# A two-layer decoder trunk on one core: input tiles on two pages in turns, gate rows in three bf16 parts, wider attention units, a new table of times

## The chip, the cores and the metric

The kernel runs on one core of one Trainium2 chip. The metric is the time of one launch on the device in microseconds, as the median of several runs. The core has a matmul engine (PE, with its weight loads shown apart as PEld), a vector engine (DVE), a scalar engine (ACT), a general engine (POOL) and a queue engine (SP) from which nearly all DMA transfers are issued. Each engine works through its own instructions strictly in order. Where an instruction needs something that another engine or a transfer produces, it waits at the head of its engine, and all that stands behind it waits too.

## The reference, cut to what matters

Input x is 1024 rows of 1024 f32. There are two layers. Each normalizes the rows, projects them by one wide matrix, runs three kinds of mixer on the columns, multiplies by gates, and projects back.

```python
for layer in range(DEPTH):                        # DEPTH = 2
    h = rms_norm(x, ln_g[layer])
    if layer % 2 == 0:
        u = h @ even_w_in[li]
        y_a = mla_mixer(...)                      # 8 heads, causal softmax attention
        y_b = nsa_mixer(...)                      # 8 heads in 2 groups: compressed, selected, window
    else:
        u = h @ odd_w_in[li]
        y_c = dsa_mixer(...)                      # top 256 keys of an indexer's score
        y_d = mlstm_mixer(...)                    # the recurrence, below
    y_m = mem_xattn(...)                          # 256 memory slots
    x = x + concat(y1 * silu(gate), y2 * silu(gate), y_m * silu(gate)) @ w_out[layer]
```

The recurrence of the second layer, for each of 4 heads, goes over chunks of the sequence with a state C (64x128), n and m:

```python
        b = jnp.cumsum(lfc, axis=-1)
        D = jnp.where(tril, b[..., :, None] - b[..., None, :] + ic[..., None, :], NEG)
        m_t = jnp.maximum(b + m[..., None], D.max(-1))
        a = jnp.exp(b + m[..., None] - m_t)
        w = jnp.einsum('bhtd,bhsd->bhts', qc, kc) * jnp.exp(D - m_t[..., None])
        num = a[..., None] * jnp.einsum('bhtd,bhdv->bhtv', qc, C) + jnp.einsum('bhts,bhsv->bhtv', w, vc)
```

## The kernel before, in words

The program first records every operation of the whole trunk (a recorder's `add`), then orders them with a list scheduler, and only then issues them. All instructions but a few therefore come from line 559, the one place that issues, and a profile row is told from another by the names of its tiles.

**What sets the order.** Each operation belongs to a segment, such as `norm` (normalizing the input tiles), `e_agate` (a block of columns of the first projection), `nsa`, `mlstm` or `dsa`. The table `SEG` gives each segment two times, between which its operations get their due times. The scheduler fills the five engines by these due times and by a planner's costs; some elementwise operations may go to DVE, ACT or POOL, by the weights in `PRICE`. Tiles live in pages of 4 KB or 2 KB for each partition; PSUM has 8 banks. A tile that is asked for when no page is free has to wait for the last reader of an older one.

**Precision.** A projection splits h and the weights into a high and a low f16 half, `hT` (h transposed by DMA, from `nh` and `nl`) and `wl`, so each product is three 512-column matmuls for each of 8 slices of the inner dimension. The row `wl,hT` is this work. It is also what the scheduler has at hand to fill PE while other chains run. Raw weights come in as `wr`, 512 KB at a time.

**The start** (`even`, class `Lazy`). The 8 tiles of 128 input rows come as `xt`, each on a page of its own, issued up to two tiles ahead of the one being normalized. For each tile ACT squares it (`nj`), POOL forms the scale (`ms`), ACT or DVE makes `nh` and DVE `nl`, and two DMA transposes write `hT`.

**The sparse attention** (`attention`, `units`). For each of 8 query tiles and 2 head groups, scores go into PSUM (by `u_S`), DVE reduces them to a row maximum (`nm`), ACT takes the exponential into `P`, and its high and low halves go to `PS`, which is turned into `PT` by the DMA (`PT<-PS`) or by PE. One unit is as many heads as fit in `UNIT` = 512 score columns:

```python
        n = 128 * grp["nk"] or 64
        per = max(1, min(4, UNIT // max(n, 128)))
```

**The recurrence** (`mlstm`). Gate pre-activations lie as `lf` and `ig` with positions on partitions. Sixteen small PE transposes (`cst,lf` and `cst,ig`) turn them into rows of 4 heads by 1024 positions. DVE then scans the rows; from these come `nu` (in the page `row0`) and `a` (in `row3`), both 4x1024 f32. To use a row against a 128-partition tile, a matmul with a 4-row selector `sel` spreads it over the partitions: `row,sel` 4x512 for `qa`, and 4x128 for each head and chunk of 128 positions (8 chunks), added in PSUM to a mask (`mb,idb`) before an exponential. These matmuls have f32 operands; the trace shows each as two instructions. The chunk ends with `mixB`, and the recurrence's state goes on to the next.

Of the kernel before, what the change touches and what calls it, by code (L numbers as in the profile page):

```python
# [10 lines left out]
BF = mybir.dt.bfloat16  # L11
# [14 lines left out]
PRICE = {"V": 0.6056, "S": -0.3, "G": -0.042}  # L26
# [636 lines left out]
def shape_constants():  # L663
# [8 lines left out]
    for i in range(NT):  # L672
# [8 lines left out]
SEG = dict(mem1=(-1964.354997, -749.898006), setup=(-1816.241273, -1509.540986), nsak=(-356.853517, 1584.760751), norm=(12.478188,  # L681
           60.715408), e_agate=(30.389285, 702.674675), kv0=(180.608921, 332.472885), cmp=(295.381558, 524.45868),
           late=(404.880094, 623.097485), q1=(414.776892, 755.823398), nsav=(449.064004, 909.7325), q0=(574.250466, 967.487664),
           e_kv1=(639.09141, 640.09141), e_lat=(657.807884, 810.40051), e_bgate=(702.751148, 801.565528), kv1=(719.691156,
           930.091156), e_bq=(742.856149, 985.342984), e_mq=(764.26877, 930.810665), e_kv2=(790.238444, 844.321004),
           nsa=(872.306006, 1320.680104), tab1=(879.7302, 1666.299134), mla0=(909.091866, 999.091866), mla1=(963.432059,
           1054.709671), oA0=(1011.102231, 1143.413799), mkv0=(1035.698803, 1135.060803), mem0=(1071.084555, 1249.633293),
           oBM0=(1130.594329, 1373.974849), topk1=(1192.612434, 1894.010943), o_idx=(1305.901793, 1411.398144),
           topk0=(1324.297644, 1929.352671), o_og1=(1349.47565, 1535.745353), o_cgate=(1373.820186, 1759.504578),
           o_dqk=(1519.607611, 1585.829092), o_og0=(1553.774079, 1798.172126), o_mq=(1729.947172, 1862.135725), o_cq=(1760.056059,  # L690
           1908.507699), o_dv=(1799.75511, 1904.957928), mlstm=(1813.754032, 2012.421441), mkv1=(1844.716227, 1889.690991),
           cv=(1879.3423, 2062.848758), dsa=(1890.783201, 2305.248509), oBM1=(1961.965806, 2207.495428), oA1=(2186.525082,
           2466.927226))
# [3 lines left out]
UNIT = 512  # L697
# [10 lines left out]
class Trunk:  # L708
# [457 lines left out]
    def units(self, grp):  # L1166
        n = 128 * grp["nk"] or 64
        per = max(1, min(4, UNIT // max(n, 128)))
        st = {64: 64, 128: 128, 256: 256}.get(n, 512)
        res = []  # L1170
        for a in range(0, 4, per):
            res.append(dict(grp=grp, heads=list(range(a, a + per)), n=n, st=st, first=(a == 0), last=(a + per == 4), turn=False))
        return res
# [128 lines left out]
    def attention(self, kind, groups, side=None):  # L1302

        seq = []
        for gi, g in enumerate(groups):
            g["gi"] = gi
            seq += self.units(g)
# [160 lines left out]
    def even(self):  # L1468
# [19 lines left out]
        class Lazy:  # L1488
# [3 lines left out]
            def get(s, i):  # L1492
                while s.n <= i:
                    j = s.n
                    with self.seg("norm"):
                        for y in range(len(xts), min(j + 3, NT)):
                            xts.append(self.page("xt"))
                            Q.dma_start(xts[y], A["x"][0, 128 * y:128 * y + 128])
                        hT.append(self.norm_T(xts[j], "hT"))
                    xts[j] = None  # L1500
# [772 lines left out]
    def mlstm(self, qkT, gif, dv_d, mix):  # L2273
# [79 lines left out]
        sel = self.page("sel", [128, 8, 128])  # L2353
        for h in range(4):
            V.tensor_copy(sel[0:4, h], self.idf[0:4, h:h + 1].to_broadcast([4, 128]))
        for j in range(2):
            for k in range(2):
                V.tensor_copy(sel[0:4, 4 + j, 64 * k:64 * k + 64], self.idf[0:4, 2 * j + k:2 * j + k + 1].to_broadcast([4, 64]))
        dcol = self.tiny(16, F, "dcol")
        t = self.psT()  # L2360
        for j in range(2):
            T.matmul(t[:, 8 * j:8 * j + 8], sel[0:4, 4 + j], dec[0:4], start=True, stop=True)
# [12 lines left out]
        for c in range(NT):  # L2375
# [15 lines left out]
            for h in range(4):  # L2391
                T.matmul(dps[:, 128 * h:128 * h + 128], sel[0:4, h], nu[:, tk], start=True, stop=False)
# [143 lines left out]
```

## Time and profile before

| | |
|---|---|
| median of 3 runs | 1490.56 us (1482.39, 1490.56, 1491.02) |
| profiled execution | 1491.9 us |
| its span | 1490.1 us (1.8 us lie outside) |
| mean granted clock of PE | 0.966 |
| PE, DVE busy | 1369.9 us (92%), 1270.4 us (85%) |
| ACT, POOL busy | 1077.0 us (72%), 459.0 us (31%) |

A busy share is an average over the whole program. The program has stretches with different limits, so the rows are read by stretch. [...]

### The profile page before, as it was taken

The numbers are of one execution on the slowest core, as the hardware profiler recorded it, in microseconds if no ns is written. First come the engines' busy times: TensorE is split into PE (matmuls) and PEld (weight loads), VectorE is DVE, ScalarE is ACT, GpSimd is POOL, SyncE is SP. The second block draws the span as 40 slices with busy tenths as digits, with TensorE's granted clock in tenths as the row PEclk, the third lists the DMA queues.
The fourth block names the chain that finished last, engine by engine and source line by source line (L and its number), as shares of the span: only waits on it lengthen the run. The fifth ranks groups of instructions, "written<-read, shape, count | busy, mean of one in ns | idle before, by whom it ended". The sixth has DMA issues, their size and how long they took to land. (4 is left out here: it accounts for less than half of the span.)

```text
span 1490.1 us, 30067 instructions
## 1 busy us (share of the span) xinstructions
PE 1369.9 (92%) x10496; PEld 784.3 (53%) x10496; DVE 1270.4 (85%) x3477; ACT 1077.0 (72%) x2497; POOL 459.0 (31%) x501
## 2 busy tenths in 40 slices
PE   3999999999888889978899999999998978999997
PEld 1345445556666556655656554444443455665553
DVE  7656798999989978798899899868999988988894
ACT  8545565558878968895888789999997565655580
POOL 1312355767420323341214310000266523221030
PEclk9999999999999999999999999999998897699999
DMA  9827522468498798978998332042135477369996
GB/s 304 203 78 176 162 86 88 121 144 165 99 178 162 148 218 213 246 180 156 213 221 163 87 89 75 15 135 82 36 91 143 89 124 216 82 152 244 264 244 159
DMA packets 441849, 225.49 MB, mean 151 GB/s; under 512 B 378080, under 2 KB 404320, under 8 KB 441696
## 3 DMA queue, kind: packets, MB, share of 16 engines
q1 hardware_dynamic: 441696, 223.57, 63.9%
q8 instruction: 82, 1.34, 0.4%
q14 instruction: 71, 0.58, 0.1%
HBM read 83.61 MB, written 46.66 MB: 87 GB/s over the span
## 5 line engine op out<-in xcount | busy, mean ns | idle before, releaser
L559 PE MATMUL psum<-wl,hT 128*128 128x512 f16 (+4 forms) x2928 | 662.8, 367 | 14.1 <-DMA hT<-nh 8.3
L559 PEld LDWEIGHTS <-hT 128*128 128x128 f16 x2928 | 279.5, 98 | 313.6 <-issue 29.7
L559 PEld LDWEIGHTS <-PT 128*128 128x128 f16 x3792 | 234.9, 101 | 74.5 <-DMA PT<-PS 44.3
L559 PE MATMUL psum<-wl,oT 128*128 128x512 f16 x960 | 265.6, 383 | 8.8 <-DVE oe L559 3.3
L559 POOL TENSOR_TENSOR ms<-ms,nhalf 128x4 f32<-128x4 f32 (+3 forms) x105 | 118.2, 1130 | 456.6 <-DVE ms L559 221.9
L559 ACT ACTIVATE P<-psum,nm 128x256 f32<-128x256 f32 (+8 forms) x348 | 203.1, 598 | 66.4 <-DVE nm L559 55.0
L559 PE MATMUL psum<-nv,PT 128*128 128x64 f16 x1584 | 177.0, 195 | 21.1 <-DMA PT<-PS 18.1
L559 DVE TENSOR_REDUCE nm<-psum 128x1 f32<-128x640 f32 (+8 forms) x216 | 161.9, 765 | 22.3 <-PE psum L559 21.3
L559 PEld LDWEIGHTS <-oT 128*128 128x128 f16 x960 | 93.6, 99 | 105.5 <-DMA oT<-osp 7.6
L559 DVE SCALAR_TENSOR_TENSOR PS<-P,PS 128x512 f16<-128x512 f32 (+6 forms) x160 | 129.3, 811 | 2.6 <-ACT PS L559 2.4
L559 PE MATMUL psum<-cst,P 128*128 128x128 f32 x502 | 103.3, 295 | 8.3 <-ACT P L559 4.2
L559 ACT ACTIVATE PT<-psum 128x512 f16<-128x512 f32 (+3 forms) x160 | 76.9, 507 | 38.6 <-PE psum L559 31.6
L559 PEld LDWEIGHTS <-qf 128*128 128x128 f16 x832 | 78.0, 101 | 43.5 <-issue 13.7
L559 PE MATMUL psum<-nkst,qf 128*128 128x320 f16 (+5 forms) x384 | 95.8, 320 | 4.0 <-DVE PT L559 1.6
L559 DVE SCALAR_TENSOR_TENSOR PT<-psum,PT 128x512 f16<-128x512 f32 (+3 forms) x160 | 88.1, 567 | 10.2 <-ACT PT L559 9.6
L559 ACT ACTIVATE tkj<-tkr,tkv 128x768 bf16<-128x768 f32 (+5 forms) x96 | 83.5, 872 | 14.2 <-DVE tkv L559 7.6
L559 ACT ACTIVATE PS<-P 128x512 f16<-128x512 f32 (+6 forms) x113 | 82.1, 729 | 4.2 <-PE psum L559 2.8
L559 ACT ACTIVATE wj<-wr 128x1024 bf16<-128x1024 f32 (+5 forms) x78 | 79.2, 1020 | 8.1 <-DMA wr<-even_w_in 5.2
L559 PE MATMUL psum<-vp,PT 128*128 128x64 f16 x864 | 79.0, 193 | 5.5 <-DMA PT<-PS 3.1
L559 PE MATMUL psum<-cvp,PT 128*128 128x64 f16 x864 | 78.0, 193 | 6.1 <-DMA PT<-PS 5.6
L559 DVE TENSOR_TENSOR wl<-wr,wl 128x1024 f16<-128x1024 f32 (+4 forms) x65 | 78.1, 1208 | 3.9 <-ACT wl L559 3.5
L559 ACT ACTIVATE tkj<-stop,tkd,tkf 128x1024 bf16<-128x1024 bf16 (+5 forms) x84 | 80.7, 967 | 0.1
(498 smaller groups left out, 2822.7 us busy)
## 6 DMA issues: line engine op xcount, KB each, us to landing
wr<-even_w_in SPq DMA_DIRECT2D x20, 512.0 KB, 5.0
wr<-w_out SPq DMA_DIRECT2D x20, 512.0 KB, 5.3
wr<-odd_w_in SPq DMA_DIRECT2D x20, 512.0 KB, 4.4
gate<-gate_d SPq DMA_DIRECT2D x32, 256.0 KB, 4.7
gate_d<-gu SPq DMA_DIRECT2D x24, 256.0 KB, 2.2
qa_d<-mqT SPq DMA_DIRECT2D x16, 384.0 KB, 2.6
xt<-x SPq DMA_DIRECT2D x8, 512.0 KB, 10.3
x<-x SPq DMA_DIRECT2D x8, 512.0 KB, 5.8
```

The source lines that it names most:

```text
L559: r = getattr(engines[o.eng], meth)(*[res(a) for a in args], **{k: res(v) for k, v in kw.items()})
```

## The change: what it does

There are four edits. The input tiles use two pages in turns: tile y goes into the page of tile y-2, and one tile is fetched ahead less. The two gate rows are each split into three bf16 rows whose sum is the f32 value to within what three bf16 mantissas hold (copy, subtract, copy, subtract), and the selector is bf16, so that each f32 matmul becomes three bf16 matmuls into the same PSUM columns; the small `dec,sel` matmuls stay f32. In the sparse attention alone a unit may have 1024 score columns, two PSUM banks. And `SEG` and one weight of `PRICE` have new numbers, so that all is ordered anew.

```diff
-PRICE = {"V": 0.6056, "S": -0.3, "G": -0.042}
+PRICE = {"V": 0.5977, "S": -0.3, "G": -0.042}
...
-           60.715408), e_agate=(30.389285, 702.674675), kv0=(180.608921, 332.472885), cmp=(295.381558, 524.45868),
+SEG = dict(mem1=(-2553.531656, -565.442386), setup=(-2429.265397, -2428.265397), norm=(0.251578, 91.068331), nsak=(60.696859,
...
-UNIT = 512
+UNIT = {"mla": 512, "nsa": 1024, "mem": 512, "dsa": 512}
...
-    def units(self, grp):
+    def units(self, grp, width):
         n = 128 * grp["nk"] or 64
-        per = max(1, min(4, UNIT // max(n, 128)))
+        per = max(1, min(4, width // max(n, 128)))
...
-                        for y in range(len(xts), min(j + 3, NT)):
-                            xts.append(self.page("xt"))
+                        for y in range(len(xts), min(j + 2, NT)):
+                            xts.append(xts[y - 2] if y > 1 else self.page("xt"))
                             Q.dma_start(xts[y], A["x"][0, 128 * y:128 * y + 128])
...
-        sel = self.page("sel", [128, 8, 128])
...
+        selb = self.page("selb", [128, 6, 128], BF)
+        sel = self.page("sel", [128, 2, 128])
...
+        def thirds(x):
+
+            res = [self.page("third", dt=BF)[0:4] for _ in range(3)]
+            r = self.page("rest")[0:4]
+            self.copy(res[0], x)
+            self.tt(r, x, res[0], OP.subtract)
+            self.copy(res[1], r)
+            self.tt(res[2], r, res[1], OP.subtract)
+            return res
+        nu3, a3 = thirds(nu), thirds(a)
...
             for c in range(2):
-                T.matmul(ps[:, c], sel[0:4, 4 + j], a[:, 512 * c:512 * c + 512], start=True, stop=True)
+                for x, r in enumerate(a3):
+                    T.matmul(ps[:, c], selb[0:4, 4 + j], r[:, 512 * c:512 * c + 512], start=(x == 0), stop=(x == 2))
...
-                T.matmul(dps[:, 128 * h:128 * h + 128], sel[0:4, h], nu[:, tk], start=True, stop=False)
+                for x, r in enumerate(nu3):
+                    T.matmul(dps[:, 128 * h:128 * h + 128], selb[0:4, h], r[:, tk], start=(x == 0), stop=False)
```

**The queue of SP at the program's start.** In the name of a row, the first word is the tile written, after the arrow what is read. Before, from its fifth row on (ahead of these stand one `xt`, `cst` of 82 KB, `gcol` of 27.5 KB and one `wr`):

```order
L559 DMA wr_116<-even_w_in 128x2x512
L559 DMA wr_120<-even_w_in 128x2x512
L559 DMA wr_122<-even_w_in 128x2x512
L559 DMA xt_124<-x 128x1024
L559 DMA xt_126<-x 128x1024
L559 DMA xt_133<-x 128x1024
L559 DMA xt_142<-x 128x1024
L559 DMA xt_163<-x 128x1024
L559 DMA xt_178<-x 128x1024
L559 DMA xt_183<-x 128x1024
L559 DMA_TRANSPOSE hT_187<-nh_168 128x8x128
```

And now, from its fifth row on (ahead stand `w` of 256 KB, `cst`, `gcol` and one `xt`):

```order
L559 DMA xt_116<-x 128x1024
L559 DMA wr_120<-even_w_in 128x2x512
L559 DMA wr_122<-even_w_in 128x2x512
L559 DMA wr_124<-even_w_in 128x2x512
L559 DMA wr_128<-even_w_in 128x2x512
L559 DMA posi_137<-pos 128x9
L559 DMA wr_148<-even_w_in 128x2x512
L559 DMA gb_160<-rows 128x968
L559 DMA mraw_172<-cst 128x896
L559 DMA_TRANSPOSE hT_181<-nh_177 128x8x128
L559 DMA_TRANSPOSE hT_191<-nl_179 128x8x128
L559 DMA xt_102<-x 128x1024
```

Six tiles of `x` moved from ahead of the first transpose to behind it, each after the transposes of an earlier tile, and three other loads and one weight tile moved ahead of it.

**PE where the recurrence's gates are turned into rows.** Before, the transposes of `lf` (`cst,lf`) stand among projection matmuls:

```order
L559 MATMUL psum<-wl_15247,hT_11029 128x512
L559 MATMUL psum<-cst_88,lf_13143 4x128
L559 LDWEIGHTS hT_12460
L559 MATMUL psum<-wl_14489,hT_12460 128x512
L559 MATMUL psum<-cst_88,lf_13143 4x128
L559 LDWEIGHTS hT_11713
L559 MATMUL psum<-wl_14806,hT_11713 128x512
```

Now they stand in one run (`mT` is the transposed memory, another projection's operand):

```order
L559 LDWEIGHTS mT_15256
L559 MATMUL psum<-wl_15586,mT_15256 128x512
L559 MATMUL psum<-cst_88,lf_13088 4x128 x8
L559 LDWEIGHTS hT_12551
L559 MATMUL psum<-wl_14573,hT_12551 128x512
```

Over the whole program, 2102 of the 512-column matmuls `wl,hT` and `wl,mT` stood ahead of the first of these transposes, and 2216 do now. From there to the recurrence's last chunk there were 298 of them, and 184 are there now; of the output projection's (`wl,oT`) there were 35 and are 4.

**PE at the gate rows of the first chunks.** Before, a row against the selector stands alone:

```order
L559 MATMUL psum<-row_3397_15563,sel_12929 128x128
L559 LDWEIGHTS hT_12065
L559 MATMUL psum<-wl_15184,hT_12065 128x512
L559 LDWEIGHTS idb_131
L559 MATMUL psum<-mb_429,idb_131 128x128
```

Now each of them is three matmuls with a weight load ahead of each. At the first chunk's last head the parts of `nu` (here `third_15847`, 128 columns) share a run of twelve with the parts of `a` (`third_16016` and `third_16033`, 512 columns), of which five rows are:

```order
L559 MATMUL psum<-third_16016,selb_15183 128x512
L559 LDWEIGHTS selb_15183
L559 MATMUL psum<-third_15847,selb_15183 128x128
L559 LDWEIGHTS selb_15183
L559 MATMUL psum<-third_16033,selb_15183 128x512
```

What moved is the place of `a`: its two matmuls for each of two tiles stood alone and ahead of all chunks, and their parts now stand in that run. In all, 36 f32 matmuls (32 of 128 columns, 4 of 512) became 108 bf16 matmuls, each with a weight load of its own; on DVE 8 copies of `sel` became 3, three subtractions or copies of 4x1024 were added, and ACT got four and POOL one. On DVE 264 row maxima became 244 and the DMA transposes `PT<-PS` went from 160 to 150.

## Rows read from the trace of the kernel before

**Rows 1.** The page: span, busy time by engine, and the ending chain by step.

```profile
span 1490.1 us, 30067 instructions
...
PE 1369.9 (92%) x10496; PEld 784.3 (53%) x10496; DVE 1270.4 (85%) x3477; ACT 1077.0 (72%) x2497; POOL 459.0 (31%) x501
...
PE psum L559 15%; DMA PT<-PS 2%; ACT P L559 1%; DVE PS L559 1%; DVE row L559 1%; DVE P L559 1%; ACT tkj L559 0%; POOL ms L559 0%; DMA oT<-osp 0%; DVE Cst L559 0%; DVE x L559 0%; ACT PS L559 0%; DVE tkn L559 0%; DVE tkr L559 0%; SPq L559 0%
```

**Rows 2.** Windows: stretch, length, busy time (instructions) by engine, clock, DMA, GB/s.

```profile
0.00:48.00 48.00, 21.07 (x75) 8.28 (x76) 35.58 (x132) 38.20 (x57) 6.72 (x13) 0.90 1.03 288
48.00:320.00 272.00, 269.56 (x1402) 136.86 (x1400) 209.92 (x756) 146.85 (x347) 122.84 (x142) 1.00 0.44 123
320.00:860.00 540.00, 485.64 (x5275) 321.37 (x5273) 483.80 (x1115) 434.39 (x1099) 186.37 (x228) 0.98 0.84 176
860.00:1111.00 251.00, 247.50 (x1198) 119.21 (x1196) 220.16 (x647) 236.62 (x478) 33.43 (x31) 1.00 0.24 74
1111.00:1142.00 31.00, 28.74 (x141) 13.24 (x139) 30.05 (x63) 26.33 (x56) 19.97 (x14) 1.00 0.45 147
1142.00:1200.00 58.00, 55.49 (x226) 26.74 (x227) 52.57 (x123) 29.89 (x65) 29.50 (x20) 0.82 0.40 86
1200.00:1330.00 130.00, 115.43 (x791) 75.97 (x789) 113.89 (x347) 82.53 (x233) 34.99 (x31) 0.83 0.67 148
1330.00:1490.00 160.00, 146.44 (x1404) 82.66 (x1399) 124.42 (x301) 82.24 (x168) 25.18 (x24) 1.00 0.96 224
```

**Rows 3.** PE's timeline at the start: start, length, work, idle before and releaser.

```profile
21.80 3.39 PE L559 MATMUL psum<-wl,hT 128*128 128x512 f16 x8 [8.26 <-DMA hT<-nh]
...
28.15 8.32 PE L559 MATMUL psum<-wl,hT 128*128 128x512 f16 x30
...
43.61 16.73 PE L559 MATMUL psum<-wl,hT 128*128 128x512 f16 x64 [1.80 <-DVE gu L559]
```

**Rows 4.** The tile xt: what reads it (ns min, median, max), and its landing.

```profile
L559 ACT ACTIVATE nj<-xt x8: 1038/1039/1057, 4.4 to 27.1; 128x1024 bf16<-128x1024 f32 x8
...
DMA to landing us min/median/max: 3.6/10.3/11.0
```

**Rows 5.** PE's timeline in the recurrence.

```profile
1118.81 21.10 PE L559 MATMUL psum<-wl,hT 128*128 128x512 f16 x97
1142.06 1.98 PE L559 MATMUL psum<-row,sel 4*128 4x512 f32 x4 [2.15 <-ACT row L559]
...
1238.64 0.48 PE L559 MATMUL psum<-row,sel 4*128 4x128 f32 x2
...
1255.17 0.79 PE L559 MATMUL psum<-row,sel 4*128 4x128 f32 x2 [3.87 <-DVE PT L559]
```

**Rows 6.** Windows of 4 us where the gate rows end (columns as in rows 2).

```profile
1140.00:1144.00 4.00, 1.94 (x4) 0.66 (x4) 4.00 (x4) 3.98 (x5) 4.00 (x2) 1.00 0.63 164
1144.00:1148.00 4.00, 2.21 (x5) 1.26 (x5) 4.00 (x9) 3.17 (x10) 2.26 (x3) 0.54 0.71 133
1148.00:1152.00 4.00, 3.34 (x12) 1.46 (x11) 4.00 (x11) 1.49 (x4) 0.00 (x0) 0.50 0.35 66
```

**Rows 7.** The tile row: its copy on DVE and an exponential on ACT.

```profile
L559 ACT ACTIVATE strow<-row x2: 1054/1055/1056, 1130.9 to 1143.1; 4x1024 f32<-4x1024 f32 x2
L559 DVE COPY row<-psum x1: 1202/1202/1202, 1116.7 to 1116.7; 4x1024 f32<-4x1024 f32 x1
```

**Rows 8.** Groups by shape: busy us, mean ns, idle before and releaser.

```profile
L559 POOL TENSOR_TENSOR wl<-wr,wl 128x1024 f16<-128x1024 f32 x19 | 44.1, 2323 | 35.9 <-ACT wl L559 23.7 <-PE psum L559 8.6 <-DVE wl L559 2.1
...
L559 PEld LDWEIGHTS <-idb 128*128 128x128 bf16 x248 | 24.8, 100 | 13.8 <-issue 1.8
...
L559 DVE TENSOR_REDUCE nm<-psum 128x1 f32<-128x1024 f32 x16 | 19.4, 1218 | 2.1 <-PE psum L559 1.9
...
L559 DVE TENSOR_REDUCE nm<-psum 128x1 f32<-128x512 f32 x24 | 16.1, 680 | 0.0
```

**Rows 9.** What PE waited for: total us, times, longest.

```profile
PE psum L559 <- DMA PT<-PS: 31.1, 32, 3.1
```

More of the change, by code (lines that the diff above doesn't have):

```diff
@@ L678, in shape_constants @@
     return c
-SEG = dict(mem1=(-1964.354997, -749.898006), setup=(-1816.241273, -1509.540986), nsak=(-356.853517, 1584.760751), norm=(12.478188,
-           60.715408), e_agate=(30.389285, 702.674675), kv0=(180.608921, 332.472885), cmp=(295.381558, 524.45868),
[L683 to L693, printed above, removed]
@@ new lines @@
+SEG = dict(mem1=(-2553.531656, -565.442386), setup=(-2429.265397, -2428.265397), norm=(0.251578, 91.068331), nsak=(60.696859,
+           1538.120436), e_agate=(171.33351, 771.686517), cmp=(174.284895, 488.621415), late=(175.937474, 604.970939),
+           q1=(410.702592, 450.538766), nsav=(473.233518, 937.172328), kv0=(496.192916, 834.479676), e_kv1=(503.492017,
+           610.61793), q0=(540.654991, 944.014504), e_lat=(657.807884, 810.40051), e_bgate=(696.328747, 795.143128),
+           e_bq=(742.856149, 919.882141), kv1=(747.606624, 990.444352), e_mq=(764.26877, 930.810665), e_kv2=(790.296979,
+           844.379539), nsa=(872.306006, 1320.680104), tab1=(892.840546, 1684.102713), mla0=(909.091866, 996.176523),
+           mla1=(991.127269, 1054.709671), mkv0=(1035.698803, 1135.060803), oA0=(1036.464838, 1142.292346), mem0=(1076.208498,
+           1254.757236), oBM0=(1133.782374, 1377.162893), topk1=(1195.995111, 1894.621025), o_idx=(1305.901793, 1418.004966),
+           o_og1=(1316.898953, 1539.059171), topk0=(1320.28138, 1929.352671), o_cgate=(1396.110474, 1780.678022),
+           o_dqk=(1537.749253, 1599.020946), o_og0=(1606.005922, 1805.340579), o_cq=(1674.294572, 1877.928297), o_mq=(1716.781976,
+           1853.081082), cv=(1745.740444, 2048.281883), mkv1=(1788.302893, 1889.866807), o_dv=(1798.083266, 1907.690467),
+           mlstm=(1815.433596, 2006.209633), oBM1=(1955.379054, 2245.360699), dsa=(1969.715907, 2284.982961), oA1=(2009.907991,
+           2828.098532))
@@ L1306, in attention @@
             g["gi"] = gi
-            seq += self.units(g)
+            seq += self.units(g, UNIT[kind])
         for x, u in enumerate(seq):
@@ L1495, in get @@
                     with self.seg("norm"):
-                        for y in range(len(xts), min(j + 3, NT)):
-                            xts.append(self.page("xt"))
+                        for y in range(len(xts), min(j + 2, NT)):
+                            xts.append(xts[y - 2] if y > 1 else self.page("xt"))
                             Q.dma_start(xts[y], A["x"][0, 128 * y:128 * y + 128])
                         hT.append(self.norm_T(xts[j], "hT"))
-                    xts[j] = None
                     s.n += 1
@@ L2351, in mlstm @@
         yield 1
-        sel = self.page("sel", [128, 8, 128])
[L2354 to L2358, printed above, removed]
+        selb = self.page("selb", [128, 6, 128], BF)
+        sel = self.page("sel", [128, 2, 128])
+        V.tensor_copy(selb[0:4, 0:4], self.idf[0:4, 0:4].unsqueeze(2).to_broadcast([4, 4, 128]))
+        for x in (sel, selb[:, 4:6]):
+            V.tensor_copy(x[0:4].rearrange("p j (k c) -> p (j k) c", k=2), self.idf[0:4, 0:4].unsqueeze(2).to_broadcast([4, 4, 64]))
+        def thirds(x):
[7 more added lines that the diff above has]
+        nu3, a3 = thirds(nu), thirds(a)
         dcol = self.tiny(16, F, "dcol")
@@ L2361, in mlstm @@
         for j in range(2):
-            T.matmul(t[:, 8 * j:8 * j + 8], sel[0:4, 4 + j], dec[0:4], start=True, stop=True)
+            T.matmul(t[:, 8 * j:8 * j + 8], sel[0:4, j], dec[0:4], start=True, stop=True)
         V.tensor_copy(dcol, t[:, 0:16])
```

## The prediction

> **What bounds the kernel now.** I read the page's busy times first, then the program cut into stretches, then PE's waits in those stretches. PE is busy 92% of the span and DVE 85%, and 15% of the ending chain is PE [rows 1]. The stretches tell more. From 48 to 320 us and from 860 to 1111 PE is busy 269.56 of 272 and 247.50 of 251 us at a granted clock of 1.00: there only less PE work shortens anything. From 320 to 860, the attention of the first layer, PE has 485.64 and DVE 483.80 of 540 us, so neither alone bounds it, and each waits for the other. At the start PE works 21.07 of 48 us. And in the recurrence, from 1142 to 1330, PE is busy 55.49 of 58 and 115.43 of 130 us, but its clock is 0.82 and 0.83 [rows 2]. So from 1142 to 1330 two things are lost: 17 us in which PE is idle (188 less 170.9), and the clock, worth 10.0 us in the first part and 19.6 in the second (busy time by one less the clock), together 30. How that clock falls is seen where the gate rows end. PE, at 1.00, works 1.94 and 2.21 us in two windows of 4, while DVE is busy in all of both; the second shows 0.54 and the third 0.50 [rows 6]. PE there waits 2.15 us for the exponential of a gate row, and later 3.87 us for DVE's `PT` [rows 5].
>
> So four things can be won: the start's idle 27 us, the 17 and the 30 of the recurrence, and part of the 54 us that PE is idle from 320 to 860.
>
> **The start.** PE's first projection matmul runs at 21.80 us, after 8.26 us for the transpose `hT<-nh` [rows 3]. Before, SP's queue has ahead of that transpose eight `xt` and four `wr` of 512 KB and some small ones, 6.25 MB; now it has two `xt`, five `wr` and 1.25 MB of others, 4.9 MB. At the 288 GB/s of the first 48 us [rows 2], 1.36 MB are 4.7 us. Against that, `w` of 256 KB stands ahead of the first `xt`, 0.9 us, and two `xt` rather than one ahead of `wr`, which can take 1.8 more if the weights come last. I take -4. The bounds are -8, the whole wait for the first transpose, and +5, which is the rotation's price. It is this: tile y's fetch now waits until `nl` of tile y-2 has read the page, and it is issued behind transposes on SP. A fetch takes 3.6 us alone and 10.3 in the crowd, and `nj` 1.04 [rows 4]. PE gets from one tile and one block of columns 24 matmuls; 64 take 16.73 us where PE runs on without a stop [rows 3], so 24 take 6.3 at that pace. If fetch, square, scale, halves and transposes of a tile (10.3 and some 8 more, by 1.04 for the square and more for each half) are covered by two tiles only, a tile comes each 9 us and PE lacks 2.7 a tile over the last two or three, some +8 against the -4. I expect the uncrowded fetch, and nothing lost.
>
> **The gate rows in bf16.** An f32 matmul of 128 columns shows as a pair of 0.48 us at full clock and 0.79 at half; two of 512 columns take 1.98 us, 0.99 each [rows 5]. Three bf16 matmuls of 128 columns need three loads of the selector, 0.10 each by the load of `idb` [rows 8], so some 0.30 to 0.33; three of 512 cost 3 by 0.2175 (97 in 21.10 us [rows 5]), 0.65. That saves 32 by 0.15 to 0.18 and 4 by 0.34, 6.2 to 7.1 us of PE. PE is busy nine tenths of this stretch but the chain passes between engines, so I credit 4. The splits are eight operations of 4x1024, four for each row: three fall to DVE at 1.20 and four to ACT at 1.05 [rows 7], one to POOL, where a larger subtract takes 2.32 [rows 8]. DVE gains 3.6 and loses five selector copies (a few tenths each, about 1): 2.6 more on an engine that is full there [rows 2, 6]. The parts of `nu` are off the path, since `nu` exists before the exponential of `a`. Those of `a` are four steps in a row, 1.05, 2.32, 1.05 and 1.20, 5.6 us, and PE's twelve matmuls in a run wait for the last; some 56 projection matmuls, 12 us, stand ahead of that run, so it is hidden unless ACT comes late with the first copy. I put +1 on the path: -3 in all. The ends are -8 (all of PE's saving and a little wait) and +7 (no saving, the chain uncovered).
>
> A row of loads bears on this: 248 loads of 128 columns take 100 ns each [rows 8]. [...] No row here has a bf16 load of 4 rows.
>
> **Two-bank units.** Units merge for tiles 1, 2 and 3 only; from 5 slices of 128 on a unit already has one head and two banks. A row maximum of 512 columns takes 680 ns and one of 1024 takes 1218 [rows 8]: 8 merges save 0.14 each, 1.1 us, and at 384 and 256 columns the other 12 save as much per unit or a little more, together some 2.9 us of DVE. ACT's exponentials are for each head and stay. DVE is nine tenths busy there [rows 2], so I take -2. Against it, a unit holds two banks of 8, and its transposes `PT<-PS`, for which PE already waits 31.1 us in 32 places [rows 9], come in larger pieces. Ends: -4, and +6 (a fifth of that wait again). That the units change where they are small, in tiles 1 to 3, keeps it short.
>
> **The new order of the recurrence.** Some 145 of 512-column fill matmuls (114 of `wl,hT` and `wl,mT` ahead of it, 31 of `wl,oT` behind it) leave the stretch from `lf` to the last chunk. At 0.2175 that is 31.5 us of full-clock work. In the stretch PE does 170.9 us at 0.825, which is 141 us of full-clock work; 109.5 are left. If clock and idle stay as they are, the stretch takes 109.5/0.825 + 17 = 150 us instead of 188, and 31.5 are paid elsewhere at full clock: 181.5, a gain of 6.5. With clock c the sum is 109.5/c + 48.5, which equals 188 at c = 0.785. So it decides at a clock that is only 0.04 below today's: under it the new order loses. Fill is what keeps PE busy there; but DVE, busy 52.57 of 58 and 113.89 of 130 [rows 2], also gives work away to the tail (the last attention's row maxima and splits), which shortens its side. In the tail DVE has 124.42 of 160 and PE 146.44, so it can take this. I take -5. The ends: at c = 0.95, 163.8, -24; at c = 0.68, 209.5, +21.
>
> **The sum.** -4 -3 -2 -5 = -14 against the profiled 1491.9, so 1478; the median lies 1.3 under the profiled time, so 1477.
>
> **The rivals.** *Nothing to measure* (1482 to 1498, I name 1489): the moved work costs the same where it goes; 24.8 of the 31.5 us are put where PE has no idle time [rows 2], and the start's and DVE's gains go to waits. Against it stands that the stretch at 0.83 pays more for the same work. Chance 0.28.
>
> *Slower, the recurrence loses its cover.* One mechanism: without the fill, PE, which issues in order, stands between chunks for DVE's steps and for the three parts; what happened at 1140 to 1152 [rows 6], half-busy windows and then 0.50, happens at each of eight chunks. With c = 0.70 the sum is 204.9, +17, and the start's and units' -6 and the chain of `a` uncovered, +5, leave +16: 1507. It decides at c = 0.785. For it: 97 projection matmuls cover the scans now [rows 5] and about 60 will; the rows of 1255.17 show the wait for DVE already. Against: DVE has less to do there too. Chance 0.18.
>
> *A larger gain.* With DVE's and PE's shares both smaller, the eight chunks follow without the 0.5 windows; c = 0.92 gives 167.5, -20, and with the others' -9: 1461. Chance 0.17. *Two pages starve PE* at the start, +8 instead of -4: 1489. Chance 0.04; it adds to the first. That the edits don't do what they say is excluded by the order of instructions; only their value is open. The forecast, 1466 to 1482, has 0.33.
>
> **How the numbers follow.** About 1% (15 us) is what a measurement of this kernel tells from no change; the three runs before spread over 8.6 us. Faster by over 1% is under 1475.7: all of the larger gain, and some two thirds of the forecast's, 0.39. Slower by over 1%, above 1505.5, is two thirds of its rival and a tail of others: 0.16. The rest is 0.45. Range: the larger gain's outer half and the slower case's outer third left out, 1452 to 1503.
>
> **What would show it.** Start: first `wl,hT` before 20 us, and PE's busy time up to 48 us above 21. Gate rows: three bf16 matmuls within 0.35 us, and PE's total busy less by some 6. Units: DVE's maxima 2.9 us less. Recurrence: from the first `lf` to the last chunk under 190 us (219 before), and its clock, which I expect at 0.80 to 0.85. I would be wrong if that clock is below 0.78 or above 0.92, if PE's wait at the run of twelve passes 5 us, or if the stretch from 860 on grows by more than the 24.8 us that it is given.

## The result, and the profile after

The changed kernel takes 1501.76 us (median of 4 runs, 1499.74 to 1508.71) against 1487.67 for the kernel before: a ratio of 1.0089, 95% interval 1.0061 to 1.0118. Measured once more (e6 below) it is 1.0063 (1.0040 to 1.0085). It is slower by 9 to 14 us, some 1%; 1477 was forecast, in a range up to 1503.

To see where, both executions are cut at the same events: 48 us, the first and the last matmul `nkst,qf` (the sparse attention), the first transpose of `lf`, the end of the last `mixB` of the recurrence. Windows of the kernel before, columns as in [rows 2], the clock as a share of full speed:

```profile
0.00:48.00 48.00, 21.07 (x75) 8.28 (x76) 35.58 (x132) 38.20 (x57) 6.72 (x13) 0.90 1.03 288
48.00:320.60 272.60, 270.16 (x1408) 137.14 (x1405) 210.52 (x758) 147.10 (x347) 123.12 (x143) 1.00 0.44 124
320.60:799.20 478.60, 425.27 (x4879) 289.56 (x4878) 429.94 (x946) 389.08 (x1000) 160.70 (x184) 0.98 0.88 184
799.20:1111.60 312.40, 307.87 (x1595) 150.98 (x1592) 274.02 (x816) 282.28 (x579) 58.83 (x76) 1.00 0.29 82
1111.60:1330.10 218.50, 199.16 (x1153) 115.77 (x1152) 196.01 (x529) 138.14 (x350) 84.45 (x64) 0.85 0.57 131
1330.10:1490.10 160.00, 146.34 (x1400) 82.60 (x1398) 124.32 (x301) 82.24 (x168) 25.18 (x24) 1.00 0.96 224
```

The same windows of the changed kernel; this execution, 1508.71 us, is the longest of its four:

```profile
0.00:48.00 48.00, 24.85 (x106) 10.88 (x107) 36.37 (x133) 33.31 (x51) 16.63 (x29) 1.00 1.06 274
48.00:321.50 273.50, 271.04 (x1415) 138.98 (x1415) 216.95 (x772) 154.26 (x349) 118.39 (x127) 0.99 0.46 127
321.50:813.30 491.80, 427.59 (x4907) 292.21 (x4906) 443.22 (x929) 390.77 (x1006) 168.60 (x190) 0.96 0.85 178
813.30:1146.20 332.90, 327.02 (x1641) 159.31 (x1640) 297.24 (x861) 298.06 (x608) 69.20 (x79) 1.00 0.33 94
1146.20:1325.50 179.30, 162.91 (x994) 97.15 (x993) 153.88 (x427) 104.41 (x279) 50.59 (x45) 0.80 0.50 120
1325.50:1506.90 181.40, 159.92 (x1476) 89.60 (x1474) 145.43 (x352) 92.62 (x191) 26.26 (x22) 0.99 0.92 205
```

And three of them of its second profile (e6, 1497.64 us), which stands nearer to the median:

```profile
321.40:805.40 484.00, 423.12 (x4906) 289.12 (x4905) 438.09 (x928) 389.86 (x1006) 168.27 (x190) 0.98 0.87 181
...
1138.70:1315.40 176.70, 160.66 (x994) 97.31 (x993) 153.77 (x427) 104.14 (x278) 50.79 (x45) 0.82 0.52 122
1315.40:1495.90 180.50, 159.89 (x1476) 89.71 (x1474) 145.95 (x351) 92.97 (x191) 27.13 (x22) 0.99 0.91 206
```

The reader is to see four things. The recurrence became 39 to 42 us shorter. The stretch ahead of it became 20.5 to 20.9 us longer and the tail 20.5 to 21.4, so that the three together moved by +2.7 (first profile) and -0.4 (second). The attention became longer by 13.2 in the one and 5.4 in the other; some 8.6 of these 13.2 are clock (busy time by one less the clock, 17.1 against 8.5; the clock is shown to 0.01, so each is good to 2 us), which differs between two executions of the same kernel. And PE's 4 us more of work up to 48 us did not let the attention begin earlier: 321.5 against 320.6. PE's total is 1373.3 and 1366.8 us, against 1369.9 [rows 1].

PE's timeline at the start of the changed kernel, against [rows 3]:

```profile
21.21 0.59 PE L559 MATMUL psum<-wl,hT 128*128 128x512 f16 x1 [4.51 <-ACT wl L559]
22.66 5.37 PE L559 MATMUL psum<-wl,hT 128*128 128x512 f16 x16 [0.86 <-DVE wl L559]
...
49.96 0.24 PE L559 MATMUL psum<-wst,oneb 128*128 128x1 bf16 x4 [3.56 <-DVE wst L559]
```

The wait for the transpose is gone and a wait for the weights' halves, `wl`, stands in its place; the first matmul comes 0.6 us earlier. PE's wait for the first part of `a` in e6 (it was 2.15 us for the f32 row in [rows 5]):

```profile
1163.17 0.79 PE L559 MATMUL psum<-third,selb 4*128 4x512 bf16 x2 [4.47 <-ACT third L559]
```

And in the first profile, with PE's timeline where the gate rows of the first chunk stand:

```profile
1171.03 1.01 PE L559 MATMUL psum<-third,selb 4*128 4x512 bf16 x2 [4.79 <-ACT third L559]
...
1183.86 0.23 PE L559 MATMUL psum<-third,selb 4*128 4x128 bf16 x1
1184.02 0.39 PE L559 MATMUL psum<-wl,hT 128*128 128x512 f16 x1
1184.34 0.23 PE L559 MATMUL psum<-third,selb 4*128 4x128 bf16 x1
1184.50 0.39 PE L559 MATMUL psum<-wl,hT 128*128 128x512 f16 x1
1184.82 0.23 PE L559 MATMUL psum<-third,selb 4*128 4x128 bf16 x1
1184.98 0.39 PE L559 MATMUL psum<-wl,hT 128*128 128x512 f16 x1
1185.20 0.22 PE L559 MATMUL psum<-mb,idb 128*128 128x128 bf16 x1
1185.26 0.38 PE L559 MATMUL psum<-wl,hT 128*128 128x512 f16 x1
1185.57 0.22 PE L559 MATMUL psum<-third,selb 4*128 4x128 bf16 x1
```

From start to start, a part and the projection matmul behind it take 0.48 us (1183.86 to 1184.34), and a projection matmul alone takes 0.2175 [rows 5]. So a part costs 0.26, where the prediction had 0.10. Of the mask, `mb,idb` with 128 rows, the neighbour follows 0.06 behind (1185.20 to 1185.26); of a part it follows 0.16 behind, and the next part 0.32 behind that.

### The profile page after: what moved, and what is told of

It is laid out like the page before. It is cut to its first block, busy times and chain, and to the rows that moved or that the text cites. A ratio compares the mean times of both kernels' runs of the same rounds, so it can differ in the third digit from the quotient of the medians.

```text
span 1506.9 us, 30133 instructions
## 1 busy us (share of the span) xinstructions
PE 1373.3 (91%) x10532; PEld 788.1 (52%) x10532; DVE 1293.1 (86%) x3467; ACT 1073.4 (71%) x2481; POOL 449.7 (30%) x490
## 5 line engine op out<-in xcount | busy, mean ns | idle before, releaser
L559 PE MATMUL psum<-wl,hT 128*128 128x512 f16 (+4 forms) x2928 | 651.8, 366 | 7.1 <-ACT wl L559 6.0
L559 PEld LDWEIGHTS <-PT 128*128 128x128 f16 x3792 | 223.4, 102 | 79.4 <-DMA PT<-PS 43.8
L559 POOL TENSOR_TENSOR ms<-ms,nhalf 128x4 f32<-128x4 f32 (+3 forms) x105 | 112.5, 1076 | 296.6 <-DVE ms L559 239.9
L559 PE MATMUL psum<-nv,PT 128*128 128x64 f16 x1584 | 162.6, 196 | 13.7 <-DMA PT<-PS 8.9
L559 DVE TENSOR_REDUCE nm<-psum 128x2 f32<-128x512 f32 (+11 forms) x196 | 160.1, 829 | 16.9 <-PE psum L559 15.7
L559 DVE SCALAR_TENSOR_TENSOR PS<-P,PS 128x512 f16<-128x512 f32 (+6 forms) x150 | 135.1, 905 | 3.4 <-ACT PS L559 3.0
L559 POOL TENSOR_TENSOR wl<-wr,wl 128x1024 f16<-128x1024 f32 (+2 forms) x29 | 63.8, 2203 | 174.7 <-DVE wl L559 116.8
L559 PE MATMUL psum<-cvp,PT 128*128 128x64 f16 x864 | 83.3, 196 | 10.8 <-DMA PT<-PS 8.2
L559 PEld LDWEIGHTS psum<-cst,P 128*128 128x128 f32 x502 | 65.8, 144 | 31.9 <-ACT P L559 12.7
L559 ACT ACTIVATE tkj<-stop,tkd,tkf 128x384 bf16<-128x384 bf16 (+5 forms) x84 | 80.6, 965 | 1.1 <-DVE tkb L559 0.9
```

The costliest lines, as they stand in the source:

```text
L559: r = getattr(engines[o.eng], meth)(*[res(a) for a in args], **{k: res(v) for k, v in kw.items()})
```

## The experiments

All ratios are to runs of the kernel before on the same chip. "In its own order" means that the instructions are ordered as in the kernel named, and only then some are replaced, doubled or left out.

**e1 to e4: the edits mixed.** The first theory was that the two-bank units made the attention longer (A), the rival that the new order did (B). e1 and e2 put the units in and out, e3 and e4 the table and the weight:

```diff
-UNIT = 512                      # e1: only this of the change; e2: all but this
+UNIT = {"mla": 512, "nsa": 1024, "mem": 512, "dsa": 512}
-SEG = dict(mem1=(-1964.354997, ...)      # e3: only this and PRICE; e4: all but these
+SEG = dict(mem1=(-2553.531656, ...)
```

> The kernel before with the two-bank units of the sparse attention alone. Theory A, the units cost the time: the first layer's attention (first to last matmul nkst,qf) grew from 478.6 to 491.8 us in the changed kernel, so this kernel shows that growth too, attention 488 to 495 us, and is slower than before by 8 to 15 us (ratio 1.005 to 1.010). Theory B, the new order costs it: the attention stays within 4 us of 478.6 and the ratio is 0.997 to 1.003.

> The changed kernel with the units of before (512 columns), all else changed. Theory A (units): it is back near the kernel before, ratio 0.997 to 1.002, attention 476 to 483 us. Theory B (order): it stays slower, ratio 1.006 to 1.011, attention above 487 us.

> The kernel before with the new table of times and the new weight alone. Theory A: within 0.3% of before. Theory B: ratio 1.005 to 1.012, and the three stretches move as in the changed kernel: first transpose of lf near 1140 to 1146 us (1111.6 before), last mixB near 1325, some 180 us of tail.

> The changed kernel with the old table of times and the old weight. Theory A: ratio 1.005 to 1.010, attention above 487 us. Theory B: ratio 0.994 to 1.003, since the three small edits together are worth -9 to +3 us by the predicted terms of start, gate rows and units.

Measured: 1.0291 (1.0269 to 1.0313), 1.0199 (1.0176 to 1.0221), 1.0357 (1.0331 to 1.0383) and 1.0429 (1.0402 to 1.0457). All four are far slower than both kernels, which neither theory had. The attention took 509.4, 492.4, 493.8 and 502.2 us; without the merged units (e2) it is no shorter than with them (491.8 and 484.0), which speaks against A. B's sizes are missed as well. But all four are ordered anew, and the next two runs show that this alone costs time; A is settled only by e9.

**e5 and e10: one weight, no operation changed.** Theory C: a table of times fits one exact program, and any change makes an order that it was not fitted to.

```diff
-PRICE = {"V": 0.6056, "S": -0.3, "G": -0.042}     # e5: kernel before; e10: the reverse, in the changed kernel
+PRICE = {"V": 0.5977, "S": -0.3, "G": -0.042}
```

> The kernel before with one number changed, the weight of DVE in PRICE from 0.6056 to 0.5977; no operation is added or taken away. Theory C, each table fits one exact program: an order made anew with the old table loses 10 to 40 us, whatever the edit, so ratio 1.007 to 1.027. Rival D, the four mixed kernels were slow because of what was in them: such a small change of a weight is worth nothing, ratio 0.997 to 1.003.

> The changed kernel with the one weight set back to 0.6056. Theory C (each table fits one exact program): slower than the changed kernel by 10 to 40 us, ratio to before 1.013 to 1.033. Rival D: 1.004 to 1.009.

Measured: e5 1.0166 (1.0139 to 1.0194), 24.5 us lost on the kernel before; e10 1.0132 (1.0113 to 1.0151), 6 to 10 us lost on the changed kernel (1.0089 and 1.0063), at the lower edge of C's range. C holds so far: an order made anew with a table of another program loses time without any edit. What e1 to e4 lost on the kernel before, 28 to 62 us, is therefore misfit and edit together and prices no edit. So the edits were then tried in a kernel's own order.

**e15: the table fitted anew.** e2's program, with `SEG` and the weight changed by a random search on its own ordering.

> The changed kernel with the units of before, as e2, but with the table of times and the weight fitted anew to this program by a random search on the program's own ordering. Theory C, the mixed kernels were slow because their table was made for another program: 15 to 28 us of e2's loss come back, ratio 0.999 to 1.010. Rival D, the units of before are what makes it slow: it stays above 1.015.

Measured: 1.0109 (1.0084 to 1.0134). Of e2's 28 us over the kernel before, 13.5 came back, a little less than C's bound; the rest may be content or an unfinished search, which this run does not tell apart.

**e6: the changed kernel again**, with no edit.

> The changed kernel once more, for a second profile beside the three next ones on this chip. Ratio 1.006 to 1.012; by stretch, attention 486 to 492 us, first lf 1138 to 1146, recurrence 176 to 182, tail 177 to 182 us.

Measured: 1.0063 (1.0040 to 1.0085), 1500.93 us; the stretches are those above. The attention, 484.0, came out under the 486 to 492 expected.

**e9: the merged units halved, in the changed kernel's own order.** Row maxima, both halves of P and the DMA transpose are each two operations of half the size.

```diff
+            if per > 1 and n in (384, 512):
+                o.real = [("tensor_reduce", (), dict(out=nm[:, b:b + 1], in_=s[:, b, 0:n], ...)) for b in range(2)]
+                o.real = [("dma_start", (pt[:, f], u["ps"][:, f]), dict(transpose=True)) for f in range(2)]
```

> The changed kernel in its own order, but in each merged unit of the sparse attention the row maximum, both halves of P and the DMA transpose are two operations of half the size again. By the prediction's term (2.9 us of DVE saved by the merging, 2 of it on the path) this kernel is 2 to 5 us slower than the changed one, ratio to before 1.008 to 1.010, with DVE busy 3 to 6 us more. If the larger pieces were what makes the attention longer (theory A in what is left of it), it is faster than the changed kernel: ratio 1.000 to 1.004, attention 479 to 482 us.

Measured: 1.0115 (1.0091 to 1.0140), with DVE busy 1293.9 us against 1287.1 in e6; both lie just past what the predicted term gave. The attention took 492.3 us, so it is not the larger pieces that made it longer: A falls. The merging is worth some 4 us by the first measurement of the changed kernel, which is not clear of the noise, and some 8 by e6. That is more than the term, which counted row maxima only, while e9 also doubles the halves of P and the transposes.

**e13: the tile loads alone, in the order of before.** Six loads of `xt` move behind the transposes in SP's queue.

```diff
+        for y in range(2, 8):
+            order.remove(xs[y])
+            order.insert(min(after + 1, first), xs[y])     # behind the transposes of tile y-2
```

> The kernel before in its own order, with six of its tile loads moved in SP's queue alone: tiles 2 to 7 of x are fetched each behind the transposes of the tile two before it (their pages stay eight). By the prediction's start term the first projection matmul comes some 4 us earlier than 21.8 and 4 us stay: ratio 0.996 to 0.999. Theory K, what the start gains is given back later: PE's busy time up to 48 us rises from 21 to 24 or 25, but the attention starts within 1 us of 320.6 and the ratio is 0.999 to 1.002.

Measured: 1.0077 (1.0054 to 1.0099), slower than both theories. PE's timeline:

```profile
16.20 0.59 PE L559 MATMUL psum<-wl,hT 128*128 128x512 f16 x1 [3.33 <-ACT wl L559]
17.46 3.15 PE L559 MATMUL psum<-wl,hT 128*128 128x512 f16 x7 [0.68 <-DVE wl L559]
36.30 0.16 PE L559 MATMUL psum<-wst,oneb 128*128 128x1 bf16 x1 [15.70 <-DVE wst L559]
```

The first projection matmul comes 5.6 us earlier, and then PE stands for 15.7. In the old order ACT has the squares of later tiles ahead of the weights' work, and waits there 13.9 us in all for loads that now come later (total, times, longest):

```profile
ACT nj L559 <- DMA xt<-x: 13.9, 6, 3.6
```

The attention starts at 330.6, 10 us late, and the kernel ends 11.6 us late: a loss at the start is paid in full. In the changed kernel the order on ACT was changed along with the loads, so this is no price of its start.

**e7 and e8: the gate rows in f32 again, in the changed kernel's own order**, first for `nu` alone, then for both rows. Of each split only one copy is left.

```diff
-                    T.matmul(dps[...], selb[0:4, h], r[:, tk], start=(x == 0), stop=False)      # three bf16 parts
+                    ... (dps[...], self_[0:4, h], full[:, tk]), dict(start=True, stop=False)    # one f32
```

> The changed kernel in its own order, but the 32 groups of three bf16 matmuls on nu are one f32 matmul each again, at the place of the first; its split is one copy; the selector for it is f32. By the prediction's term (0.48 against 0.30 to 0.33 us, 32 times, on a path that is half PE's) the f32 kernel is 3 to 5 us slower than the changed one. Theory E, three loads and three passes cost what one f32 pair costs: within 1.5 us of the changed kernel. Theory F, the three parts' chain holds PE up: the f32 kernel is faster by 3 to 6 us.

> The changed kernel in its own order, with both gate rows in f32 again: 36 f32 matmuls at the place of the first of three bf16 ones, each split only one copy. Theory E (three bf16 matmuls cost what an f32 pair costs, nothing else): ratio to before 1.004 to 1.007, as the changed kernel's 1.0063. Theory F (the parts of a hold PE up; PE waited 4.5 to 4.8 us for the second part in both profiles of the changed kernel): that wait is gone, the recurrence is 172 to 174 us rather than 176.7 to 179.3, and the ratio is 1.000 to 1.003. By the prediction's term the bf16 rows gain, and this kernel is 3 us slower than the changed one: 1.008.

Measured: e7 1.0041 (1.0023 to 1.0059), e8 1.0085 (1.0062 to 1.0108), on either side of e6. Neither differs from the changed kernel (1.0063 and 1.0089) by more than the noise, so three spread 4-row bf16 matmuls cost the kernel what one f32 matmul does (E) to within some 3 us; a smaller gain or loss these runs can't tell. F falls: in e8 PE still waits 4.6 us, for ACT's first copy, so it is not the later parts that hold it up. PE's timeline of e7, from one head's gate row to the next:

```profile
1175.81 0.48 PE L564 MATMUL psum<-full,self 4*128 4x128 f32 x2
...
1177.25 0.48 PE L564 MATMUL psum<-full,self 4*128 4x128 f32 x2
```

PEld's timeline in e6 shows why a part is dear: the selector's load starts with its matmul, 0.23 us after the load ahead has ended, while that of `idb` starts 0.01 us after the start of the load ahead of it, and 0.22 us before its own matmul at 1174.84.

```profile
1173.97 0.09 PEld L559 LDWEIGHTS <-selb 4*128 4x128 bf16 x1 [0.23 <-issue]
1174.12 0.10 PEld L559 LDWEIGHTS <-hT 128*128 128x128 f16 x1
1174.45 0.09 PEld L559 LDWEIGHTS <-selb 4*128 4x128 bf16 x1 [0.23 <-issue]
1174.61 0.10 PEld L559 LDWEIGHTS <-hT 128*128 128x128 f16 x1
1174.62 0.10 PEld L559 LDWEIGHTS <-idb 128*128 128x128 bf16 x1
```

**e11, e14 and e17: other forms of the same rows, in the changed kernel's own order.** Theory J: a 4-row load beside 128-row weights is not hidden. e14 and e17 change the rows of `nu` alone, e11 those of `a` as well.

```diff
+ # e11: one matmul; the parts lie at partitions 0, 32 and 64 of one tile, the selector has ones in all three places
+ ("matmul", (dps[...], selp[:, h], packs[0][:, tk]), dict(start=True, stop=False))
+ # e14: three matmuls, each part in a tile of 128 partitions with zeros elsewhere, the selector of 128 rows
+ ("matmul", (dps[...], selp[:, h], packs[min(x, 1)][:, tk]), dict(start=(x == 0), stop=False))
+ # e17: the three 4-row matmuls of the change one behind another
+ [("matmul", (dps[...], selb[0:4, h], p[:, tk]), dict(start=(p is nu3[0]), stop=False)) for p in nu3] * (x == 2)
```

> The changed kernel in its own order, with the three bf16 parts of a gate row laid in one tile at partitions 0, 32 and 64 (zeros elsewhere) against one 128-row selector that has ones in all three places: one bf16 matmul in place of three, and its weights have 128 rows. What the traces show: in the changed kernel a head's three parts with four projection matmuls and the mask take 1.71 us (0.48 for each part with its neighbour, against 0.2175 for the neighbour alone), in the kernel with f32 nu the same place takes 1.44; the selector's load starts only when the matmul ahead of it has ended, while the 128-row load of idb starts early. Theory J, a 4-row load stands in the open: here the same place takes 1.0 to 1.1 us, and as 32 of these save up to 0.65 us the recurrence is 8 to 18 us shorter than 176.7; ratio 0.996 to 1.002. Theory E, PE's share at these places is not on the path: ratio 1.004 to 1.008.

> The changed kernel in its own order, with three bf16 matmuls for each use of nu as it has them, but the parts lie in tiles of 128 partitions (zeros elsewhere) and the selector's load has 128 rows. The third part is left out and the second is added twice. Theory J, the 4-row load is what costs: a head's place takes 1.0 to 1.15 us rather than 1.71, and the kernel comes within 4 us of the one with a single packed matmul (0.9958): ratio 0.995 to 1.000. Rival L, the number of matmuls costs: 1.4 us and more for the place, ratio 1.003 to 1.008.

> The changed kernel in its own order, but the three 4-row parts on nu stand one behind another at the place of the third, where they stood among projection matmuls in the first chunks; nothing is left out. Theory J2, only the step between a 128-row and a 4-row weight is dear, once for a run of three: the first chunk's place falls from 1.71 to 1.3 to 1.45 us, and the kernel gains 1 to 6 us on the changed one: ratio 1.002 to 1.006. Theory J3, each 4-row load is dear wherever it stands: 1.6 us and more, ratio 1.006 to 1.009.

PE's timeline of e14 (a part, its neighbour, the next part, and the first part of the next head), then of e17, then of e11:

```profile
1177.36 0.22 PE L562 MATMUL psum<-pack,selp 128*128 128x128 bf16 x1
1177.41 0.38 PE L562 MATMUL psum<-wl,hT 128*128 128x512 f16 x1
1177.63 0.22 PE L562 MATMUL psum<-pack,selp 128*128 128x128 bf16 x1
...
1178.44 0.22 PE L562 MATMUL psum<-pack,selp 128*128 128x128 bf16 x1
```

```profile
1176.95 0.34 PE L560 MATMUL psum<-third,selb 4*128 4x128 bf16 x3
...
1178.24 0.34 PE L560 MATMUL psum<-third,selb 4*128 4x128 bf16 x3
```

```profile
1175.94 0.22 PE L562 MATMUL psum<-pack,selp 128*128 128x128 bf16 x1
...
1176.91 0.22 PE L562 MATMUL psum<-pack,selp 128*128 128x128 bf16 x1
```

From one head's gate row to the next, with four projection matmuls (0.87 us by themselves) and a mask between, at full clock:

| gate row of a head | place, us | recurrence, us | ratio to before |
|---|---|---|---|
| three 4-row bf16, spread (e6) | 1.71 | 176.7 | 1.0063 (1.0040 to 1.0085) |
| one f32 (e7) | 1.44 | 177.9 | 1.0041 (1.0023 to 1.0059) |
| three 4-row bf16 in a row (e17) | 1.29 | 170.6 | 1.0016 (0.9999 to 1.0033) |
| three 128-row bf16, spread (e14) | 1.08 | 166.1 | 0.9980 (0.9963 to 0.9997) |
| one 128-row bf16 (e11) | 0.97 | 163.9 | 0.9958 (0.9943 to 0.9974) |

J is shown: with as many matmuls, at the same places, 128 rows rather than 4 take the place from 1.71 to 1.08 and the kernel down by some 0.8%. The load and the moved part change their rows together in e14, so which of the two makes the difference is seen only in when the loads start (PEld in e6 above, and in e14 below). L falls; J2 holds over J3, with a little more gained than it said. e11 is the fastest kernel here, 7.4 us under the kernel before and some 16 to 20 under the changed one. PEld in e14, the load of the part whose matmul starts at 1177.63:

```profile
1177.41 0.10 PEld L562 LDWEIGHTS <-selp 128*128 128x128 bf16 x1
```

The recurrence of e11:

```profile
1139.30:1303.20 163.90, 133.31 (x921) 83.06 (x921) 152.96 (x427) 106.12 (x280) 50.43 (x45) 0.89 0.55 131
```

PE has 27 us less than in e6, the clock is 0.89, and DVE with 153 of 164 us is now the busiest engine.

**e12 and e16: gate rows in the order of before.** e12 packs two f16 parts into one 128-row matmul; e16 has three 4-row bf16 matmuls in a row on `nu`.

```diff
+ [("T", "matmul", (dps[...], selp[:, h], pn[:, tk]), dict(start=True, stop=False))]                                       # e12
+ [("T", "matmul", (dps[...], selp[0:4, h], r[0:4, tk]), dict(start=r is pn, stop=False)) for r in (pn, pa, pa)]            # e16
```

> The kernel before in its own order, with each gate row in two f16 parts (a copy and a subtraction) laid in one tile at partitions 0 and 32, against one 128-row f16 selector: 36 single f16 matmuls in place of 36 f32 ones. Theory J: an f32 row matmul between projections costs 0.48 to 0.52 us, this one 0.05 to 0.1, so 32 by 0.4 and 4 by 0.75, up to 16 us of PE in the recurrence (at half clock more), 5 to 14 of it in the time; ratio 0.990 to 0.997. Theory E: ratio 0.998 to 1.003.

> The kernel before in its own order, where each of the 32 uses of nu is three 4-row bf16 matmuls one behind another in place of one f32 matmul, with one copy on ACT and one subtraction on DVE for the parts (two parts; the second stands in for the third as well, which is left out). By the prediction's term the place costs 0.30 to 0.33 us in place of 0.48: ratio 0.996 to 1.000. Theory M, in the old order the recurrence is bound by DVE (196 us of 218) and not by PE, so gate rows are worth little whatever they cost: 0.998 to 1.004, as the packed one, which took 23 us off PE, was worth 0.1%.

Measured: e12 0.9989 (0.9971 to 1.0007), e16 1.0005 (0.9992 to 1.0018). e12 misses J's range. It took PE from 1369.9 to 1347.0 us; the recurrence became only 6.6 us shorter (211.9, with DVE busy 198.1 of them), and in the whole, by the medians, 2.3 us came out. M holds in both forms: in the old order the rows were worth nothing clear of the noise. That DVE is why fits its busy time there and was not tried by itself.

## Why the prediction was wrong, point by point

By stretches, e6 against the kernel before: up to the attention +0.8 us, the attention +5.4, all behind it -0.4, together +5.8. The forecast had -4, -2 and -8 for the same three.

**The start, -4 forecast.** Half right. Idle time and clock in the first 48 us fell from 29.0 to 23.2 us, but the step "nothing lost" failed: the attention did not start earlier. By its start PE had done 38 more matmuls (x106 and x1415 against x75 and x1408), by the trace all `wl,hT` of 512 columns: fill that the new order had taken out of the recurrence, 8.3 us at 0.2175. So the time that the start won was filled with moved work. This is read from the counts and was not tried by itself. The feared starving by two pages did not come.

**Gate rows, -3 forecast.** The step that failed is the price "0.10 each by the load of `idb`", some 0.30 to 0.33 for three. The load does take 0.09, but it is not hidden (it starts with its own matmul, e6 at 1174.45), and 0.26 is what a part costs where the new order spreads the parts among projections. In a row they cost 0.42 with the mask (1.29 less 0.87) and some 0.36 without, close to the forecast. So in the changed order the edit was worth nothing clear of the noise (e7 and e8), and in the old one too (e16). The exposed wait for `a` came from ACT's first copy, the case that the prediction had named ("unless ACT comes late with the first copy"): 4.5 to 4.8 us against 2.15 before, 2.3 to 2.6 more where +1 was put. By itself a load took 0.09 us with 4 rows and 0.10 with 128 (PEld in e6): the rows show in when it starts and not in how long it takes.

**Units, -2 forecast.** Right in sign; 4 to 8 us by e9, with DVE's 6.8. DVE's row maxima took 160.1 us against 161.9, 1.8 less where 2.9 was forecast.

**The new order, -5 forecast.** This is the main failure, and the step is "31.5 are paid elsewhere at full clock". What the recurrence gives back came as worked out. From the first gate row to the last `mixB` the prediction had 150 us instead of 188 (1142.06 to 1330.1); it took 154.5 (1171.03 to 1325.5) and, in e6, 152.2 (1163.17 to 1315.4). From `lf` on it became 39 to 42 us shorter, at a clock of 0.80 to 0.82. But 41 to 42 us were paid elsewhere. Ahead of `lf` 20.5 to 20.9 were paid where 24.8 were charged: by the trace 95 more matmuls of the fill stand there (38 more ahead of the attention, 19 fewer in it), 20.7 us at 0.2175, so the price of these was right. The tail was charged 6.7 us and grew by 20.5 to 21.4: in e6 13.6 of PE's work and 7 of idle time, as DVE there went from 124.32 to 145.95 us. The charge counted the output projection, `wl,oT`, alone. PE's groups from 1330 us on, before:

```profile
L559 PE MATMUL psum<-wl,oT 128*128 128x512 f16 x426 | 112.3, 380 | 2.9 <-DMA oT<-osp 2.9
L559 PE MATMUL psum<-cvp,PT 128*128 128x64 f16 x789 | 73.2, 193 | 6.1 <-DMA PT<-PS 5.6 <-DVE mixA L559 0.2
L559 PE MATMUL psum<-ckst,qf 128*128 128x384 f16 (+4 forms) x132 | 36.0, 329 | 0.0
L559 PE MATMUL psum<-cst,P 128*128 128x128 f32 x51 | 11.0, 297 | 0.4 <-ACT P L559 0.4
```

And from 1315.4 us on in e6:

```profile
L559 PE MATMUL psum<-wl,oT 128*128 128x512 f16 x448 | 120.0, 384 | 2.7 <-DMA oT<-osp 2.0 <-DVE mixA L559 0.7
L559 PE MATMUL psum<-cvp,PT 128*128 128x64 f16 x800 | 79.0, 193 | 10.9 <-DMA PT<-PS 8.4 <-DVE mixA L559 1.1 <-DVE PT L559 0.7
L559 PE MATMUL psum<-ckst,qf 128*128 128x512 f16 (+4 forms) x158 | 41.9, 331 | 0.5 <-DVE nm L559 0.3
L559 PE MATMUL psum<-cst,P 128*128 128x128 f32 x64 | 13.5, 288 | 2.1 <-DVE oe L559 1.8 <-DVE x L559 0.4
```

Of 72 more matmuls only 22 are `wl,oT`; 50 belong to the last attention, whose work the prediction moved to the tail for DVE ("row maxima and splits") but not for PE. So "it can take this" failed too.

That 150 came so near is partly luck. The 145 were counted from `lf` on but taken out of 1142 to 1330 alone. By the trace 37 of them left the stretch between `lf` and the first gate row, where PE ran at 1.00 [rows 2], and the pieces of the last attention, not counted, left in their place.

The sum also had no term for what the new order does to the sparse attention. In six profiles that keep the changed order and its units (e6, e7, e8, e11, e14, e17) it took 483.8 to 485.9 us, and 491.8 in the first profile, against 478.6 before (476.0 and 478.9 in e16 and e12), though its units had become cheaper and 19 fill matmuls had left it: by difference the new order costs some 9 to 15 us there. Why is open; no run isolates it.

Of the rivals, "slower", 1507, lay nearer by its number than 1489, but its mechanism did not come: the clock was 0.80 to 0.82 and not 0.70. "Nothing to measure" had the reason that did, that moved work costs the same where it goes. None of the three signs by which the prediction would be wrong is seen (clock, the wait at the run of twelve, 24.8 us ahead): they watched the recurrence and the stretch ahead of it, not the tail and the attention. Of its signs of being right, the length and clock of the recurrence came; the first `wl,hT` before 20 us, three parts within 0.35 us and 6 us less of PE's work did not. Had the parts had 128 rows, the changed kernel would have been faster than before (e11, e14).

## What to carry to other kernels

Price an instruction with its neighbours: the same small matmul cost 0.05 to 0.12 us (e11, e17) or 0.26 (e6), by the rows of its weights and by what stood beside it, and here the scheduler that spread it among others made the dear case the common one. Stacking the parts of a split operand along the contraction dimension, with ones in the selector for each, turns three matmuls into one and pads the load at once: in e11 a place took 0.97 us against 1.71.

Where a fitted table sets the order, taking an edit out and ordering anew measures the table's misfit along with the edit (up to 62 us lost here, with edits worth 0 to 8 in a fixed order). Fix the order first, then replace instructions in it.

Work that is moved out of a waiting stretch is paid for where it goes. Count all that moves, on every engine: here the fill alone made 31.5 us, and 41 were paid, since pieces of the last attention had moved along with it and PE waited more among them.

## What the runs showed of the hardware that was not expected

In e6 a 4-row bf16 weight load beside 128-row weights started only 0.32 us after the matmul ahead had started (1173.65 and 1173.97), and the 128-row load behind it only with the matmul that needs it (1174.12 and 1174.13): 0.48 us from part to part. The end of the matmul ahead, which is modelled, stands at 1174.04 in the trace, so "only when the matmul ahead of it has ended", as the expectation of e11 has it, is not shown to the letter. With 128 rows the same part makes 0.27 (e14, 1177.36 to 1177.63), of which 0.2175 is the neighbour's own; there the load, at 1177.41, starts together with the matmul ahead and 0.22 us before its own. The load of `idb`, which has 128 rows and stands between 128-row weights, started 0.22 us before its matmul in e6 too (1174.62 and 1174.84). Why the 4-row load started later, no run here shows.

Two executions of one kernel differed by some 8.6 us of clock in the attention alone (17.1 and 8.5 at clocks of 0.96 and 0.98), so a single profile tells less than its windows seem to.
